# Low parts of six weight units: a negation on ScalarE and an adding transfer in the place of a subtraction on VectorE

## The chip, the cores and the metric

The kernel runs on one core of a Trainium2 chip. The core has five engines that run side by side and wait for one another by semaphores: TensorE (PE) multiplies matrices, VectorE (DVE) and ScalarE (ACT) work elementwise, GpSimd (POOL) does small elementwise work and issues transfers, and SyncE (SP) issues transfers. Sixteen DMA engines carry the transfers of all queues. The metric is the device time of one execution in microseconds, as the median of several runs.

## The reference, cut to what matters

Two decoder layers over 512 tokens of width 1024, all in float32. Each layer is an attention part and a gated feed-forward part with a causal convolution of width 3:

```python
def conv_ffn(h, w_up, conv_w, conv_b, w_down):
    u = causal_dwconv(h @ w_up, conv_w, conv_b)
    gate, up = jnp.split(u, 2, axis=-1)
    return (jax.nn.silu(gate) * up) @ w_down

for i in range(DEPTH):                       # DEPTH = 2
    ...                                      # attention part, x = x + rms_norm(h, post_g)
    h = conv_ffn(rms_norm(x, ffn_pre_g[i]), ffn_w_up[i], ffn_conv_w[i], ffn_conv_b[i], ffn_w_down[i])
    x = x + rms_norm(h, ffn_post_g[i])
```

The up projection `h @ w_up` has 1024 x 5632 weights: 22 blocks of 128 gate channels and 22 of 128 up channels. The down projection has 2816 x 1024.

## The kernel before

**Split numbers.** A float32 product is made of three matmuls. Every operand is held as a high part, which is the value rounded to the float32r type, and a low part, which is the value less its high part. `mm3` (L380 to L386) issues high by high (L384), low by high (L385 here, by operand order) and high by low (L386). So each weight needs two tiles, `wh` and `wl`, of 128 x 1024.

**Weight units.** The class `Weights` takes the weights in a fixed list of units. A unit is first loaded by SP into a raw tile `wraw` (`load`, L56), then split. ScalarE writes the high part with a copy that rounds, VectorE writes the low part with one subtraction. Where a unit is made in one go (`_emit` and `split`, L88 and L89) both stand together; in the feed-forward part the two steps are called apart, as `cast` (L100) and `low` (L111), at places written into the block's code, so that they fall between other work. `wh` and `wl` have five buffers each, `wraw` three (while some other tiles are free, five). A raw tile comes free when the subtraction has read it, and that lets SP issue the next load; SP issues its loads strictly in the order of the program.

**The up projection.** Of the 22 pairs of blocks in a layer, positions 4 to 19 are made by a scheme of seven products from sums of blocks (`seven`), whose weight sums POOL makes beforehand in HBM by adding transfers. Positions 0 to 3 and 20, 21 are plain: one unit for the gate block, one for the up block, 24 matmuls of 512 columns each (`plain`). Each pair is then convolved by `evict`: ScalarE scales (L506), VectorE adds the other two taps from PSUM (L510), ScalarE takes the silu (L515), VectorE multiplies (L519, L530). Sums and differences of the results (L537 to L544) and their high and low parts (`gh`, L548, and `gl`, L552) feed the down projection.

**The down projection** works on eleven pairs of weight blocks. For each pair SP loads a whole block `a` and one half of a second block `b` (L411). VectorE makes three differences of them (L404, L404, L407), and both are then split (L88, L89). The first difference reads both loads:

```python
sub(b[:, hi], b[:, lo], a[:, hi])     # L404, needs both loads
sub(a[:, hi], a[:, hi], a[:, lo])
add(b[:, lo], b[:, hi], a[:, lo])     # L407
```

**Order.** Outside of a few hand-written stretches a scheduler sets the order in which each engine gets its instructions when the program is built. Each engine then runs its list strictly in order. Tile names with numbers (`wl_5121`) are single buffers of one unit; a number names the same thing on all engines of one program.

**The stretch of this case** is the end of the up projection in each layer: at about 380 to 440 us in layer 0 and 890 to 950 us in layer 1. There the last block of seven products, the four plain units of positions 20 and 21, and the first units of the down projection follow each other. In layer 0 of the kernel before, the four plain units are `wh_5086`, `wh_5120`, `wh_5190` and `wh_5196` with their low parts.

Of the kernel before, what the change touches and what calls it, by code (L numbers as in the profile page):

```python
# [9 lines left out]
F32 = mybir.dt.float32  # L10
F32R = mybir.dt.float32r
BF16 = mybir.dt.bfloat16
AF = mybir.ActivationFunctionType
ALU = mybir.AluOpType
# [24 lines left out]
SEVEN = range(4, 20), range(4, 20)  # L39
# [6 lines left out]
class Weights:  # L46
# [7 lines left out]
        self.extra = []  # L54

    def load(self, raw=None):  # L56
        src, w = self.units[len(self.raws)]
        if raw is None and len(self.raws) % 5 < len(self.extra):
            raw = self.extra[len(self.raws) % 5]
        if raw is None:  # L60
            raw = self.raw_pool.tile([P, 1024], F32, tag="wraw", name="wraw", bufs=3)
        if isinstance(src, tuple):
            for n, part in enumerate(src):
                self.nc.sync.dma_start(raw[:, n * S:(n + 1) * S], part())
        else:
            self.nc.sync.dma_start(raw[:, :w], src)
        self.raws.append(raw)

    def _emit(self):
        n = len(self.made)  # L70
        if callable(self.units[n]):
            self.raws.append(None)
            self.made.append(self.units[n]())
            return
        if len(self.raws) == n:
            self.load()
        w = self.units[n][1]
        raw, self.raws[n] = self.raws[n], None
        h, l = self.pair()
        self.split(h, l, raw, w)  # L80
        self.made.append((h, l))

    def pair(self):
# [3 lines left out]
    def split(self, h, l, raw, w):  # L87
        self.nc.scalar.copy(h[:, :w], raw[:, :w])  # L88
        self.nc.vector.tensor_tensor(l[:, :w], raw[:, :w], h[:, :w].bitcast(F32), ALU.subtract)  # L89

    def cast(self):
        n = len(self.made) + len(self.open)
        if callable(self.units[n]):
            self.open.append(None)
            return
        if len(self.raws) == n:
            self.load()
        h, l = self.pair()
        w = self.units[n][1]
        self.nc.scalar.copy(h[:, :w], self.raws[n][:, :w])  # L100
        self.open.append((h, l, w))

    def low(self):
        unit = self.open.pop(0)
        if unit is None:
            self._emit()
            return
        h, l, w = unit
        n = len(self.made)
        raw, self.raws[n] = self.raws[n], None  # L110
        self.nc.vector.tensor_tensor(l[:, :w], raw[:, :w], h[:, :w].bitcast(F32), ALU.subtract)  # L111
        self.made.append((h, l))

    def ahead(self, n):
# [11 lines left out]
def trunk(tc, A, out):  # L126
# [3 lines left out]
    with ExitStack() as top:  # L130
# [79 lines left out]
        def up_blocks(layer):  # L210

            def block(i, j):
                if j < 4:
                    return A[f"ffn_up_q{layer}"][j, i * P:(i + 1) * P]
                c, i = PLACE[layer][i]
                return sums_of[layer][j - 4][c][i * P:(i + 1) * P]

            parts = [lambda i=i, j=j: block(i, j)
                     for i, j in ([(0, 0)] + [(i + (j == 0), j) for i in range(PAIRS[layer])
                                              for j in (4, 1, 5, 0, 6, 7, 3)]) if i < PAIRS[layer]]  # L220
            return [(tuple(parts[n:n + 2]), S * len(parts[n:n + 2])) for n in range(0, len(parts), 2)]

        def ffn_units(layer):
            up = []
            for f in range(NF):
                if f == SEVEN[layer][0]:
                    up += up_blocks(layer)
                elif f not in SEVEN[layer]:
                    up += [(A["ffn_w_up"][layer, f, z], 1024) for z in range(2)]
            return (up + [lambda n=n: down[layer](n) for n in range(4 * HF)])  # L230

        down, later_sums = {}, []
# [5 lines left out]
        for h in range(1, 4):  # L238
            units += [(A["ev_w_dqk"][h, z], 1024) for z in range(2)]
        units += [(A["ev_w_out"][k], 1024) for k in range(3, KD)]  # L240
        units += ffn_units(0)
        units += [(A["od_w_v"][u], 1024) for u in range(4)]
        units += [(A["od_w_sqk"][u], 1024) for u in range(4)]
        units += [(A["od_w_dqk"][u], 1024) for u in range(4, 12)]
        units += [(A["od_w_dqk"][u], 1024) for u in range(4)]
        units += [(A["od_w_v12"][u], 1024) for u in range(4)]
        units += [(A["od_w_out"][k], 1024) for k in range(2, 4)]
        units += ffn_units(1)
        W = Weights(nc, wpool, units, 5)

# [204 lines left out]
        def ffn(layer, xnT, pending, written, final):  # L455
            with ExitStack() as es:
# [126 lines left out]
                def seven(n, last):  # L583
# [15 lines left out]
                    if heavy:  # L599
                        cast()  # L600
                        tap(1, 1)
                        tap(0, 2)
                        ACT.copy(p5, p)
                        low()
                        silu()
                        cast()
                        tap(1, 2)
                    else:
                        ACT.copy(p5, p)
                        low()  # L610
                        cast()
                        tap(0, 2)
                        silu()
                        tap(1, 1)
# [3 lines left out]
                    if heavy:  # L618
                        rest[0]()
                        cast()  # L620
                    else:
                        tap(1, 2)
                        cast()
                        low()
# [1778 lines left out]
```

## Time and profile before

| | |
|---|---|
| median of 3 runs | 1041.91 us (1041.2 to 1042.88) |
| profiled execution | 1040.69 us, of which the span of the profile is 1038.9 us |
| PE busy | 1029.5 us, 99% |
| DVE busy | 900.9 us, 87% |
| ACT busy | 655.0 us, 63% |
| POOL busy | 124.4 us, 12% |
| granted TensorE clock | 0.999 |
| transfers | 217.26 MB, mean 209 GB/s |
| low parts by VectorE | x112 at 1218 ns (L89, two shapes) and x132 at 1219 ns (L111) |

Matmuls are pipelined: a 512-column matmul is shown with about 380 ns, but the next one starts about 216 ns after it, so a lost time of PE shows in the distance between two starts, and less than the full loss is shown as idle. An elementwise instruction that follows another without a wait starts some 90 ns before the former's shown end. "Idle before" names the event that ended the wait last. Transfers are shown at their issue, with the time from issue to landing.

### The profile page before, as it was taken

How to read it: one execution, taken by the hardware profiler on the slowest of the kernel's cores; microseconds unless marked ns; L12 is line 12 of the kernel's file. 1: busy time of each engine (PE TensorE's matmuls, PEld its weight loads, DVE VectorE, ACT ScalarE, POOL GpSimd, SP SyncE). 2: the span in 40 equal slices, each digit the busy share in tenths (PEclk: the TensorE clock that was granted, in tenths of full speed). 3: DMA queues.
4: the chain of work that ended last, by engine and by line, in shares of the span. 5: the costliest groups of instructions: out<-in, count | busy, mean ns of one | idle time of the engine just before them, and what ended most of it. 6: DMA issues, size and time to landing. Idle time of an engine off the chain costs nothing.

```text
span 1038.9 us, 18116 instructions
## 1 busy us (share of the span) xinstructions
PE 1029.5 (99%) x6736; PEld 934.9 (90%) x6736; DVE 900.9 (87%) x1542; ACT 655.0 (63%) x1129; POOL 124.4 (12%) x245
## 2 busy tenths in 40 slices
PE   9999999999999999999999999999999999999997
PEld 9878888899999999888888888899999999988886
DVE  7998786599999999999984775659999999999897
ACT  7676676466777766647654654656667776656562
POOL 3211144221000000000032111014100000000002
PEclk9999999999999999999999999999999999999999
DMA  7897999468665564455528999678986646545452
GB/s 281 268 246 217 263 303 277 131 222 229 202 195 164 191 182 154 154 168 180 211 79 296 281 292 290 209 221 269 270 235 211 187 161 204 163 134 180 151 214 82
DMA packets 72746, 217.26 MB, mean 209 GB/s; under 512 B 10065, under 2 KB 11217, under 8 KB 64465
## 3 DMA queue, kind: packets, MB, share of 16 engines
q1 hardware_dynamic: 61728, 147.55, 41.9%
q0 software_dynamic: 9920, 67.12, 25.0%
q10 hardware_dynamic: 1008, 1.43, 0.5%
q8 instruction: 53, 0.87, 0.3%
q14 instruction: 37, 0.30, 0.1%
HBM read 208.69 MB, written 73.43 MB: 272 GB/s over the span
## 4 chain that ended last, share of the span: by engine, by line
PE 88%; DVE 8%; issue 2%; ACT 1%; POOL 0%; DMA 0%; POOLq 0%; DVEq 0%; ACTq 0%
PE u L385 11%; PE u L384 11%; PE u L386 10%; PE acc L385 5%; PE acc L386 5%; PE acc L384 5%; PE apt L384 3%; PE apt L385 3%; PE apt L386 3%; DVE wl L89 2%; PE ao L384 2%; PE ao L386 2%; PE ao L385 2%; DVE y L510 2%; PE aqk L384 1%
## 5 line engine op out<-in xcount | busy, mean ns | idle before, releaser
L384 PE MATMUL u<-xh,wh 128*128 128x256 f32 (+1 forms) x640 | 189.8, 297 | 0.3 <-ACT wh L100 0.3
L385 PE MATMUL u<-xl,wh 128*128 128x256 f32 (+1 forms) x640 | 189.6, 296 | 0.0
L386 PE MATMUL u<-xh,wl 128*128 128x256 f32 (+1 forms) x640 | 189.3, 296 | 0.0
L89 DVE TENSOR_TENSOR wl<-wraw,wh 128x1024 fp32r<-128x1024 f32 (+1 forms) x112 | 135.0, 1218 | 33.7 <-ACT wh L88 33.5
L111 DVE TENSOR_TENSOR wl<-wraw,wh 128x1024 fp32r<-128x1024 f32 x132 | 159.4, 1219 | 1.5 <-ACT wh L100 1.5
L88 ACT CAST wh<-wraw 128x1024 fp32r<-128x1024 f32 (+1 forms) x112 | 115.0, 1044 | 58.6 <-PE apt L385 11.8
L100 ACT CAST wh<-wraw 128x1024 fp32r<-128x1024 f32 x132 | 136.9, 1044 | 22.6 <-PE u L385 6.9
L510 DVE SCALAR_TENSOR_TENSOR y<-u,cw,y 128x511 f32<-128x511 f32 (+1 forms) x176 | 126.1, 744 | 1.7 <-ACT y L506 0.7
L384 PEld LDWEIGHTS u<-xh,wh 128*128 128x128 f32 x640 | 122.5, 191 | 4.2 <-ACT wh L100 0.9
L385 PEld LDWEIGHTS u<-xl,wh 128*128 128x128 f32 x640 | 122.5, 191 | 3.9 <-DVE xl L316 0.4
L386 PEld LDWEIGHTS u<-xh,wl 128*128 128x128 f32 x640 | 122.5, 191 | 3.4
L384 PE MATMUL u<-gh,wh 128*128 128x256 f32 x384 | 105.7, 275 | 0.0
L385 PE MATMUL u<-gl,wh 128*128 128x256 f32 x384 | 105.6, 275 | 0.0
L386 PE MATMUL u<-gh,wl 128*128 128x256 f32 x384 | 105.6, 275 | 0.0
L385 PE MATMUL acc<-wl,gh 128*128 128x512 f32 (+1 forms) x234 | 88.6, 379 | 0.1
L384 PE MATMUL acc<-wh,gh 128*128 128x512 f32 (+1 forms) x234 | 88.4, 378 | 0.1
L386 PE MATMUL acc<-wh,gl 128*128 128x512 f32 (+1 forms) x234 | 88.3, 377 | 0.0
L506 ACT ACTIVATE y<-u,cw 128x512 f32<-128x512 f32 x88 | 66.6, 776 | 31.1 <-PE u L386 29.4
L265 POOL TENSOR_TENSOR rv<-ms,epst 128x1 f32<-128x1 f32 x31 | 8.6, 276 | 566.4 <-ACT junk L333 269.6
L384 PEld LDWEIGHTS u<-gh,wh 128*128 128x128 f32 x384 | 73.7, 192 | 0.2 <-DVE u L617 0.2
L385 PEld LDWEIGHTS u<-gl,wh 128*128 128x128 f32 x384 | 73.7, 192 | 0.0
L386 PEld LDWEIGHTS u<-gh,wl 128*128 128x128 f32 x384 | 73.7, 192 | 0.0
(418 smaller groups left out, 2532.7 us busy)
## 6 DMA issues: line engine op xcount, KB each, us to landing
ws<-in_ffn_up_q POOLq DMA_DIRECT2D x48, 768.0 KB, 13.0
wraw<-ws SPq DMA_DIRECT2D x128, 256.0 KB, 3.0
wraw<-in_ffn_up_q SPq DMA_DIRECT2D x96, 256.0 KB, 3.0
wraw<-in_ffn_w_down SPq DMA_DIRECT2D x44, 512.0 KB, 3.5
ws<-ws POOLq DMA_DIRECT2D x16, 768.0 KB, 13.0
ws<-in_ffn_up_q POOLq DMA_DIRECT2D x24, 512.0 KB, 6.9
wraw<-in_ffn_w_up SPq DMA_DIRECT2D x24, 512.0 KB, 4.8
wraw<-in_od_w_dqk SPq DMA_DIRECT2D x12, 512.0 KB, 9.5
```

Source lines behind the costliest of these rows:

```text
L88: self.nc.scalar.copy(h[:, :w], raw[:, :w])
L89: self.nc.vector.tensor_tensor(l[:, :w], raw[:, :w], h[:, :w].bitcast(F32), ALU.subtract)
L100: self.nc.scalar.copy(h[:, :w], self.raws[n][:, :w])
L111: self.nc.vector.tensor_tensor(l[:, :w], raw[:, :w], h[:, :w].bitcast(F32), ALU.subtract)
L265: POOL.tensor_tensor(v[:, :n], ms, eps[:, :n], ALU.add)
L384: PE.matmul(o, lh, rh, start=first, stop=False, skip_group_check=more)
L385: PE.matmul(o, lh, rl, start=False, stop=False, skip_group_check=more)
L386: PE.matmul(o, ll, rh, start=False, stop=last, skip_group_check=more)
L506: ACT.activation(y[:, z], u[z], AF.Identity, bias=c[:, 3:4], scale=c[:, 2:3])
L510: DVE.scalar_tensor_tensor(y[:, z, d:], u[z][:, :S - d], c[:, 2 - d:3 - d], y[:, z, d:], ALU.mult, ALU.add)
```

## The change

For units 41, 42 and 43 of each layer's up projection (the up block of position 20 and both blocks of position 21) the low part is no longer made by VectorE. ScalarE makes the high part as before. Then it writes the negated high part into the low tile, and POOL issues a transfer that reads the same weights from HBM a second time and adds them into the low tile. The values are the same: the low part is the weight less its high part. Unit 40, the gate block of position 20, is left as it was.

```diff
@@ class Weights
     def _emit(self):
...
         h, l = self.pair()
-        self.split(h, l, raw, w)
+        if len(self.units[n]) > 2:
+            self.send(n, h, l, raw)
+        else:
+            self.split(h, l, raw, w)
...
+    def send(self, n, h, l, raw):
+        src, w = self.units[n][:2]
+        self.nc.scalar.copy(h[:, :w], raw[:, :w])
+        self.nc.scalar.activation(l[:, :w], h[:, :w].bitcast(F32), AF.Identity, scale=-1.0)
+        self.nc.gpsimd.dma_start(l[:, :w], src, accum_op=ALU.add)
     def cast(self):
...
-        self.nc.scalar.copy(h[:, :w], self.raws[n][:, :w])
+        if len(self.units[n]) > 2:
+            self.send(n, h, l, self.raws[n])
+            w = 0
+        else:
+            self.nc.scalar.copy(h[:, :w], self.raws[n][:, :w])
         self.open.append((h, l, w))
     def low(self):
...
-        self.nc.vector.tensor_tensor(l[:, :w], raw[:, :w], h[:, :w].bitcast(F32), ALU.subtract)
+        if w:
+            self.nc.vector.tensor_tensor(l[:, :w], raw[:, :w], h[:, :w].bitcast(F32), ALU.subtract)
@@ def ffn_units(layer)
-                    up += [(A["ffn_w_up"][layer, f, z], 1024) for z in range(2)]
+                    sent = [("sent",) if n > 2 * SEVEN[layer][-1] + 2 else () for n in (2 * f, 2 * f + 1)]
+                    up += [(A["ffn_w_up"][layer, f, z], 1024, *sent[z]) for z in range(2)]
```

All lines below the class move down by up to 15 in the changed program, so L404 there is L419, L411 is L426, L510 is L525, L552 is L567.

The first place is ScalarE at the end of the up projection of layer 0, where the high parts of the last three units are made. Before:

```order
L100 CAST wh_5120<-wraw_5118 128x1024
L88 CAST wh_5190<-wraw_5188 128x1024
L506 ACTIVATE y_5066<-u_5001,cw_2662 128x512
L548 CAST gh_5164<-y_4684 128x1024
L506 ACTIVATE y_5066<-u_5002,cw_2662 128x512
L88 CAST wh_5196<-wraw_5194 128x1024
```

Of the change:

```order
L96 CAST wh_5120<-wraw_5118 128x1024
L97 ACTIVATE wl_5121<-wh_5120 128x1024
L96 CAST wh_5191<-wraw_5189 128x1024
L97 ACTIVATE wl_5192<-wh_5191 128x1024
L521 ACTIVATE y_5066<-u_5001,cw_2662 128x512
L563 CAST gh_5165<-y_4684 128x1024
L521 ACTIVATE y_5066<-u_5002,cw_2662 128x512
L96 CAST wh_5198<-wraw_5196 128x1024
L97 ACTIVATE wl_5199<-wh_5198 128x1024
```

Each of the three casts is followed by its negation; the rest keeps its order.

The second place is VectorE over the same time, from the low part of unit 40 (`wl_5087`) to the first difference of the down projection's weights (`wraw_5231` before, `wraw_5234` in the change). Before:

```order
L111 TENSOR_TENSOR wl_5087<-wraw_5084,wh_5086 128x1024
L519 TENSOR_TENSOR y_4935<-y_4935 128x512
L634 TENSOR_TENSOR u_5002<-u_5002,y_5066 128x256
L111 TENSOR_TENSOR wl_5121<-wraw_5118,wh_5120 128x1024
L89 TENSOR_TENSOR wl_5191<-wraw_5188,wh_5190 128x1024
L552 TENSOR_TENSOR gl_5165<-y_4684,gh_5164 128x1024
L510 SCALAR_TENSOR_TENSOR y_5066<-u_5001,cw_2662,y_5066 128x511
L89 TENSOR_TENSOR wl_5197<-wraw_5194,wh_5196 128x1024
L510 SCALAR_TENSOR_TENSOR y_5066<-u_5001,cw_2662,y_5066 128x510
L510 SCALAR_TENSOR_TENSOR y_5066<-u_5002,cw_2662,y_5066 128x511
L404 TENSOR_TENSOR wraw_5231<-wraw_5231,wraw_5229 128x512
```

Of the change:

```order
L125 TENSOR_TENSOR wl_5087<-wraw_5084,wh_5086 128x1024
L534 TENSOR_TENSOR y_4935<-y_4935 128x512
L649 TENSOR_TENSOR u_5002<-u_5002,y_5066 128x256
L567 TENSOR_TENSOR gl_5166<-y_4684,gh_5165 128x1024
L525 SCALAR_TENSOR_TENSOR y_5066<-u_5001,cw_2662,y_5066 128x511
L419 TENSOR_TENSOR wraw_5234<-wraw_5234,wraw_5232 128x512
L525 SCALAR_TENSOR_TENSOR y_5066<-u_5001,cw_2662,y_5066 128x510
L525 SCALAR_TENSOR_TENSOR y_5066<-u_5002,cw_2662,y_5066 128x511
```

The three subtractions are gone, and the first difference of the down projection now stands two taps earlier.

The third place is SP's list of loads: the four last loads of the up projection and the first of the down projection, with what each waits for (a raw tile that comes free). Before:

```order
L66 DMA wraw_5188<-in_ffn_w_up 128x1024 [waits DMAHW0_49,DMAHW7_49,DVE_49,Activation_49]
L66 DMA wraw_5194<-in_ffn_w_up 128x1024 [waits DMAHW1_49,DVE_49]
L411 DMA wraw_5229<-in_ffn_w_down 128x1024 [waits DMAHW2_49,DVE_49]
L411 DMA wraw_5231<-in_ffn_w_down 128x512 [waits DMAHW3_49,DVE_49]
L411 DMA wraw_5305<-in_ffn_w_down 128x1024 [waits DMAHW4_49,DVE_49]
```

Of the change:

```order
L66 DMA wraw_5189<-in_ffn_w_up 128x1024 [waits DMAHW0_49,DMAHW7_49,DVE_49,Activation_49]
L66 DMA wraw_5196<-in_ffn_w_up 128x1024 [waits DMAHW2_49,Activation_49]
L426 DMA wraw_5232<-in_ffn_w_down 128x1024 [waits DMAHW1_49,DVE_49]
L426 DMA wraw_5234<-in_ffn_w_down 128x512 [waits DMAHW3_49,Activation_49]
L426 DMA wraw_5308<-in_ffn_w_down 128x1024 [waits DMAHW4_49,Activation_49]
```

The order is the same, but the load of the last up unit waits for the cast of `wh_5120`, that of `wraw_5232` for the subtraction of `wl_5087`, and the next two for the casts of `wh_5191` and `wh_5198`.

More of the change, by code (lines that the diff above doesn't have):

```diff
@@ L56, in load @@
     def load(self, raw=None):
-        src, w = self.units[len(self.raws)]
+        src, w = self.units[len(self.raws)][:2]
         if raw is None and len(self.raws) % 5 < len(self.extra):
```

## The prediction

> **What bounds the kernel now.** The chain of waits comes first, and behind it the busy shares:
>
> ```profile
> PE 1029.5 (99%) x6736; PEld 934.9 (90%) x6736; DVE 900.9 (87%) x1542; ACT 655.0 (63%) x1129; POOL 124.4 (12%) x245
> PE 88%; DVE 8%; issue 2%; ACT 1%; POOL 0%; DMA 0%; POOLq 0%; DVEq 0%; ACTq 0%
> ```
>
> PE ends nearly every wait. To gain time, the change has to remove idle time of PE; to lose time it has only to make some. So I read the stretch of the change by engine (length, PE, PEld, DVE, ACT, POOL with counts, then granted clock, DMA share, GB/s), two windows in each layer:
>
> ```profile
> 398.00:424.00 26.00, 25.70 (x141) 22.78 (x140) 24.92 (x35) 14.58 (x20) 0.00 (x0) 1.00 0.37 129
> 424.00:450.00 26.00, 25.95 (x120) 22.12 (x119) 25.86 (x36) 15.34 (x19) 0.00 (x0) 1.00 0.54 178
> 905.00:931.00 26.00, 26.00 (x142) 23.13 (x142) 24.99 (x37) 14.76 (x20) 0.00 (x0) 1.00 0.39 130
> 931.00:957.00 26.00, 25.89 (x119) 22.06 (x119) 25.86 (x36) 15.26 (x19) 0.00 (x0) 1.00 0.52 179
> ```
>
> DVE is as full as PE, with 0.14 us free in 26 from 424 on. ACT has 11 us free, POOL all, the clock is full, and the DMA engines are busy for half of the time or less. The next question is how much PE loses behind the change. In its timeline (start, length) I looked for starts further apart than 0.216 us:
>
> ```profile
> 428.29 0.38 PE L386 MATMUL acc<-wh,gl 128*128 128x512 f32 x1
> 428.65 0.45 PE L384 MATMUL acc<-wh,gh 128*128 128x512 f32 x1
> 428.94 0.38 PE L385 MATMUL acc<-wl,gh 128*128 128x512 f32 x1
> 439.74 0.38 PE L384 MATMUL acc<-wh,gh 128*128 128x512 f32 x1
> 440.17 0.48 PE L385 MATMUL acc<-wl,gh 128*128 128x512 f32 x1
> 440.49 0.38 PE L386 MATMUL acc<-wh,gl 128*128 128x512 f32 x1
> ```
>
> From 428.29 to 428.94 two starts take 0.65 instead of 0.43: 0.22 lost. From 439.74 to 440.49 they take 0.75: 0.32 lost. That is 0.53 us in layer 0, and the same two places of layer 1 (935.6 and 947.1) lose 0.61 by the same sum. Both end on DVE, the first on a tap and the second on a low part:
>
> ```profile
> 427.76 0.74 DVE L510 SCALAR_TENSOR_TENSOR y<-u,cw,y 128x510 f32<-128x510 f32 x1
> 438.89 1.22 DVE L89 TENSOR_TENSOR wl<-wraw,wh 128x1024 fp32r<-128x1024 f32 x1
> ```
>
> So **all that an earlier DVE can give here is 1.1 us**, a tenth of a per cent. In the other direction there is no such bound: its 1.1 us of idle time in the first window (26.00 less 24.92) all lie ahead of 404.5, so each microsecond by which DVE is late behind that point comes out at PE near 428 (935 in layer 1).
>
> **What goes away.** Three subtractions per layer, here with what stands between them (VectorE, layer 0):
>
> ```profile
> 402.00 1.22 DVE L111 TENSOR_TENSOR wl<-wraw,wh 128x1024 fp32r<-128x1024 f32 x1
> 403.13 1.22 DVE L89 TENSOR_TENSOR wl<-wraw,wh 128x1024 fp32r<-128x1024 f32 x1
> 404.50 1.23 DVE L552 TENSOR_TENSOR gl<-y,gh 128x1024 fp32r<-128x1024 f32 x1
> 405.64 0.74 DVE L510 SCALAR_TENSOR_TENSOR y<-u,cw,y 128x511 f32<-128x511 f32 x1
> 406.30 1.22 DVE L89 TENSOR_TENSOR wl<-wraw,wh 128x1024 fp32r<-128x1024 f32 x1
> 407.44 1.40 DVE L510 SCALAR_TENSOR_TENSOR y<-u,cw,y 128x510 f32<-128x510 f32 x2
> 408.75 0.68 DVE L404 TENSOR_TENSOR wraw<-wraw 128x512 f32<-128x512 f32 x1
> ```
>
> Three times 1.14 us (403.13 to the next start it allows, 406.30 to 407.44) would be 3.4 us. Two of the three stand ahead of `gl`, and `gl` needs `gh` of ACT:
>
> ```profile
> 401.30 1.05 ACT L88 CAST wh<-wraw 128x1024 fp32r<-128x1024 f32 x1 [1.80 <-PE u L385]
> 402.76 0.78 ACT L506 ACTIVATE y<-u,cw 128x512 f32<-128x512 f32 x1 [0.41 <-PE u L386]
> 403.44 1.03 ACT L548 CAST gh<-y 128x1024 fp32r<-128x1024 f32 x1
> ```
>
> The cast at 401.30 is let go by PE, which the change doesn't move. A negation now follows it. It is not in the trace; the nearest row is the cast of the same shape, 1.04 us. So: cast to 402.35, negation to 403.4, scaling 0.68, `gh` from some 404.0 to 405.05, `gl` at 405.07, which is 0.57 later than before. Then the tap (1.14 later) and 0.66 later, at **406.87**, the first difference of the down weights, L419. Before, two taps of 1.31 us together stood ahead of it, so 408.75 less 1.31 = **407.44** is the start at which all behind runs as before. The lead is 0.57 us. In layer 1 the same sum goes from these rows (ACT, then DVE):
>
> ```profile
> 908.12 1.05 ACT L88 CAST wh<-wraw 128x1024 fp32r<-128x1024 f32 x1 [1.93 <-PE u L385]
> 911.44 1.22 DVE L552 TENSOR_TENSOR gl<-y,gh 128x1024 fp32r<-128x1024 f32 x1
> 915.68 0.68 DVE L404 TENSOR_TENSOR wraw<-wraw 128x512 f32<-128x512 f32 x1
> ```
>
> `gl` comes at about 911.9, L419 at 913.7, and even is 914.37: a lead of 0.7. Both leads are larger than what PE loses in their layer, so with the loads in time the gain would be those 0.53 + 0.61 = 1.1 us.
>
> **The loads of L419.** It reads two loads of SP: 512 KB, then 256 KB. Before, they took (issue, us to landing):
>
> ```profile
> wraw<-in_ffn_w_down SPq DMA_DIRECT2D x1, 512.0 KB, 4.2
> ```
> ```profile
> wraw<-in_ffn_w_down SPq DMA_DIRECT2D x1, 256.0 KB, 3.7
> ```
>
> They were issued at 403.24 and 404.38, and the second landed at 408.1, 0.6 us ahead of L404. Now the first waits for the subtraction of `wl_5087` (it ends at 401.15), the second for the cast that ends at 402.35 (909.17 in layer 1). At 3.7 us the second would be there at 406.1, in time.
>
> But just then POOL's three new transfers of 512 KB are under way: they are issued behind the negations, the first at some 400.9, the second at 403.7. What an adding transfer does to a load beside it is shown earlier in the program, where POOL makes weight sums. First such a transfer alone, then a load alone, then two fences with both beside each other, and a window that counts the packets of the two queues (packets, MB, share of the time):
>
> ```profile
> ws<-in_ffn_up_q POOLq DMA_DIRECT2D x1, 512.0 KB, 5.3
> ```
> ```profile
> wraw<-ws SPq DMA_DIRECT2D x1, 256.0 KB, 2.7
> ```
> ```profile
> ws<-in_ffn_up_q POOLq DMA_DIRECT2D x1, 512.0 KB, 6.7
> wraw<-ws SPq DMA_DIRECT2D x1, 256.0 KB, 6.6
> ```
> ```profile
> ws<-in_ffn_up_q POOLq DMA_DIRECT2D x1, 512.0 KB, 8.0
> wraw<-ws SPq DMA_DIRECT2D x1, 256.0 KB, 4.8
> wraw<-in_ffn_up_q SPq DMA_DIRECT2D x1, 256.0 KB, 7.2
> ```
> ```profile
> q0 software_dynamic: 49, 0.39, 79.0%
> q1 hardware_dynamic: 43, 0.08, 9.5%
> ```
>
> A load of 256 KB alone takes 2.7 (at 300 us); beside adding transfers 6.6 (at 230.5), 4.8 and 7.2 (at 744). In the window, 2.75 us at 766, the two queues get about as many packets, 49 and 43, but POOL's hold the engines for 79% of the time and SP's for 9.5%. A load gets one small packet for each long one. I take 6.6 to 7.2 us for the second load, by the two rows nearest in kind (256 KB, beside adding transfers that follow one another): from the end of the cast at 402.4 it lands at 402.4 + 6.6 to 7.2 = 409.0 to 409.6, **1.6 to 2.2 us late**; in layer 1 at 915.8 to 916.4, 1.4 to 2.0 late. The bounds are 3.7 (in time) and 8.0 (3.0 and 2.8 late).
>
> This is the place for a rule. The Trainium skill, *DMA: Bandwidth & Descriptors*, section *Queues, rings and completion order*, has each engine take turns between the queues that have work, packet by packet; 49 against 43 agrees. It speaks against the change. By that rule, with new packets of half the length of those at 766 (an estimate), the second load would land near 410.3, and the sum would be about 5.5 in place of 3.6.
>
> What DVE then loses: it waits at L419, and the two taps behind it, which gave PE no trouble, and all that follows come as late as L419 does, 1.9 and 1.7 us in the middle. No idle time of DVE is left until 450 to take it back, so PE stops near 428 and near 935 for that much more.
>
> **The adding transfers themselves.** An addition into on-chip memory isn't in the trace. The bounds are the plain load, 4.2, and the 8.0 above. PE uses the first such low part here, in its first L386:
>
> ```profile
> 408.64 0.38 PE L385 MATMUL u<-xl,wh 128*128 128x512 f32 x1
> 408.86 0.38 PE L386 MATMUL u<-xh,wl 128*128 128x512 f32 x1
> ```
>
> From 400.9 that allows 8.0 us: enough by all rows, barely by the longest. The second is due at about 414.0, the third at 419.2, with 10 us or more each. I take nothing for it.
>
> **At nothing.** The negations (3 of 1.04 per layer) lie in ACT's free time but for the 0.57 counted above; without that cover they would cost 3.1 per layer. POOL's issues, 0.8 each in such rows, have an idle POOL under them; a busy one would push each transfer by its issue. SP's load of the last up unit goes 1.6 us earlier, and nobody waits for it. PE's order is the same.
>
> **The sum.** 1040.69 of the profiled execution + 1.9 + 1.7 = 1044.3; the median of the runs is 1.22 above that execution, so 1045.5. This case's own range is 1043.5 (0.8 late in each layer, a load of 5.8 us) to 1048 (a load of 8.0 in both layers: 1040.69 + 3.0 + 2.8 + 1.22 = 1047.7).
>
> **Rivals.**
> *A gain.* The loads aren't held back: both land in the time before 407.44 and 914.37, that is within 5.0 us. For it speaks the row of 4.8, one of three loads beside adding transfers, and that the first load leaves 2 us earlier. Against it speak 6.6 and 7.2. PE's 1.1 us at the four places go: 1040.8.
> *No change.* The loads are late by 0 to 1 us: the lead is gone and little more. This needs 5.0 to 6.0 us, between the rows. 1041.9 to 1043.9, in the middle 1042.5.
> *The adding transfer is the stall.* If an addition into on-chip memory lasts 12 us under three of its kind and the loads, PE waits at 408.86 for 4 us in each layer (the point from which it decides is 8 us); DVE's lateness hides under that. 1041.9 + 8 = 1050. For it speaks the 8.0; against it, that in the rows the longest also had company.
> The first of these is the one on the other side: one mechanism, decided at L419, with its point at 5.0 us.
>
> **How the numbers follow.** Loads held back 0.50; gain 0.14; no change 0.24; adding transfer late 0.12. A measurement of this kernel tells some 0.2%, 2.1 us, from no change. The gain of 0.1% would read as no change, so faster gets only 0.05. The rest of the gain (0.09), the no-change case (0.24) and 0.04 from the lower end of the first case make 0.37 for the same. The rest of the first case (0.46) and the last rival (0.12) make 0.58 for slower. The range from 1040.7 to 1048.6 holds the gain's value, no change, and the first case with its upper bound; it leaves out most of the last rival above and some of the gain below, together no more than 0.2.
>
> **What would show it.** In the groups: L125 with 130 instructions in place of 132, L92 with 108 in place of 112. In the table of transfers a row of six from the up weights into `wl` on POOL's queue, with 6 to 8 us; at 12 the last rival is right. DVE idle for about 3 us ahead of `gl`, put down to ACT; then L419 idle for about 2 us twice, put down to the load of the down weights. If L419 starts at 406.9 without a wait, the gain is right and PE's stalls near 428.6 and 440.2 are gone; if PE waits at 408.9 for a transfer of POOL's, the last rival. PE otherwise loses some 2 us near 430 and near 937. Wrong altogether would be a total above 1050 or a stall ahead of 400.

## The result, and the profile after

The change makes the kernel slower: **1054.6 us** median of 5 runs (1052.33 to 1056.93) against 1041.91 us (1041.18 to 1043.19), a ratio of 1.0122 (95% interval 1.0107 to 1.0138), or 12.7 us. The forecast was 1045.5, with a range up to 1048.6: the side was right, the size was not.

The profiled execution took 1056.51 us, with a span of 1054.7. Its busy shares, then the transfers that the change adds, from the table of DMA issues (count, KB each, median us from issue to landing):

```profile
PE 1034.0 (98%) x6736; PEld 938.3 (89%) x6736; DVE 895.8 (85%) x1536; ACT 661.0 (63%) x1135; POOL 129.3 (12%) x251
```
```profile
wl<-in_ffn_w_up POOLq DMA_DIRECT2D x6, 512.0 KB, 9.3
```

Six instructions less on DVE, six more on ACT and on POOL, as written. The transfers take 9.3 us in the middle, above the 8.0 that the prediction had as their upper bound. The groups show the subtractions of the weights down to 130 and 108:

```profile
L125 DVE TENSOR_TENSOR wl<-wraw,wh 128x1024 fp32r<-128x1024 f32 x130 | 156.9, 1219 | 1.8 <-ACT wh L113 1.7
L92 DVE TENSOR_TENSOR wl<-wraw,wh 128x1024 fp32r<-128x1024 f32 (+1 forms) x108 | 130.0, 1216 | 32.9 <-ACT wh L91 32.5
```

VectorE's timeline in layer 0, around the first difference of the down weights, and then the same instruction in layer 1:

```profile
401.85 0.43 DVE L649 TENSOR_TENSOR u<-u,y 128x256 f32<-128x256 f32 x1
405.19 1.23 DVE L567 TENSOR_TENSOR gl<-y,gh 128x1024 fp32r<-128x1024 f32 x1 [2.91 <-ACT gh L563]
406.34 0.74 DVE L525 SCALAR_TENSOR_TENSOR y<-u,cw,y 128x511 f32<-128x511 f32 x1
413.08 0.69 DVE L419 TENSOR_TENSOR wraw<-wraw 128x512 f32<-128x512 f32 x1 [6.00 <-DMA wraw<-in_ffn_w_down]
```
```profile
928.32 0.69 DVE L419 TENSOR_TENSOR wraw<-wraw 128x512 f32<-128x512 f32 x1 [7.03 <-DMA wraw<-in_ffn_w_down]
```

The 2.9 us of idleness ahead of `gl` and the wait for the load of the down weights are where the prediction put them; the wait is 6.0 and 7.0 us long and not 2. TensorE's timeline shows what becomes of it:

```profile
409.79 0.48 PE L401 MATMUL u<-xh,wl 128*128 128x512 f32 x1 [0.64 <-DMA wl<-in_ffn_w_up]
...
428.79 0.46 PE L399 MATMUL acc<-wh,gh 128*128 128x512 f32 x1 [1.69 <-DVE y L525]
...
434.44 0.45 PE L399 MATMUL acc<-wh,gh 128*128 128x512 f32 x1 [2.82 <-DVE y L525]
```

First a short wait for the first transferred low part, then two waits for taps that VectorE does late. And behind the second one the granted clock falls to half, which no rival had (windows; columns as in the prediction):

```profile
434.00:436.00 2.00, 1.56 (x6) 1.40 (x7) 1.90 (x5) 0.00 (x0) 0.00 (x0) 0.88 0.69 258
436.00:438.00 2.00, 2.00 (x6) 1.55 (x6) 1.97 (x4) 1.70 (x2) 0.00 (x0) 0.50 0.38 131
438.00:440.00 2.00, 2.00 (x9) 1.69 (x8) 2.00 (x2) 2.00 (x4) 0.00 (x0) 0.77 0.44 135
```

TensorE runs the same 6736 matmuls in the same order in all kernels here, so the start of the n-th matmul in one profile less that of the n-th before gives the shift at every place. The steps of that shift, in us:

| step, at its time in the kernel before | layer 0 | layer 1 |
|---|---|---|
| wait for the first transferred low part (409; 916) | 0.91 | 1.66 |
| the two waits for late taps (429; 936) | 5.04 | 5.23 |
| half clock behind them | 1.40 | 1.37 |
| stall of the kernel before that is gone (440; 947) | -0.32 | -0.32 |

That is 15.0 of the 15.8 us by which the two profiles differ. (The profiled execution of the change was 1.9 us above its median, that of the kernel before 1.2 below.) A second profile of the change (e11_change_again, below) has the two waits for late taps in both layers and the half clock in layer 1 only.

### The profile page after: what moved, and what is told of

Read it like the earlier page. It is cut to its first block, busy times and chain, and to the rows that moved or that the text cites. A ratio compares the mean times of both kernels' runs of the same rounds, so it can differ in the third digit from the quotient of the medians.

```text
span 1054.7 us, 18121 instructions
## 1 busy us (share of the span) xinstructions
PE 1034.0 (98%) x6736; PEld 938.3 (89%) x6736; DVE 895.8 (85%) x1536; ACT 661.0 (63%) x1135; POOL 129.3 (12%) x251
## 4 chain that ended last, share of the span: by engine, by line
PE 43%; DVE 3%; DMA 1%; issue 1%; ACT 1%; POOL 1%; POOLq 0%; DVEq 0%; ACTq 0%
PE u L399 5%; PE u L400 5%; PE u L401 5%; PE acc L399 3%; PE acc L400 3%; PE acc L401 3%; PE apt L399 3%; PE apt L400 3%; PE apt L401 3%; PE apv L399 1%; PE apv L401 1%; PE apv L400 1%; DMA wraw<-in_ffn_w_down 1%; DVE wl L92 1%; PE p L400 1%
## 5 line engine op out<-in xcount | busy, mean ns | idle before, releaser
L125 DVE TENSOR_TENSOR wl<-wraw,wh 128x1024 fp32r<-128x1024 f32 x130 | 156.9, 1219 | 1.8 <-ACT wh L113 1.7
L92 DVE TENSOR_TENSOR wl<-wraw,wh 128x1024 fp32r<-128x1024 f32 (+1 forms) x108 | 130.0, 1216 | 32.9 <-ACT wh L91 32.5
L91 ACT CAST wh<-wraw 128x1024 fp32r<-128x1024 f32 (+1 forms) x108 | 111.1, 1044 | 61.1 <-PE apt L400 11.7
L525 DVE SCALAR_TENSOR_TENSOR y<-u,cw,y 128x511 f32<-128x511 f32 (+1 forms) x176 | 126.0, 744 | 1.3 <-ACT y L521 0.4
L205 POOL DMA_DIRECT2D ws<-in_ffn_up_q x72 | 50.4, 722 | 166.0 <-DMA ws<-ws 61.4
## 6 DMA issues: line engine op xcount, KB each, us to landing
ws<-in_ffn_up_q POOLq DMA_DIRECT2D x48, 768.0 KB, 12.7
ws<-ws POOLq DMA_DIRECT2D x16, 768.0 KB, 12.4
```

Source lines behind the costliest of these rows:

```text
L205: nc.gpsimd.dma_start(tiles[j][c][:].rearrange(wide, q=4), src.rearrange(wide, q=4), accum_op=op, max_dma_last_dim=8192)
L525: DVE.scalar_tensor_tensor(y[:, z, d:], u[z][:, :S - d], c[:, 2 - d:3 - d], y[:, z, d:], ALU.mult, ALU.add)
```

## The experiments

Two theories stood against each other in the first runs: **A**, the transfers fill the DMA engines and the down loads come late; **B**, the negations ahead of `gh` and the moved VectorE list cost the time. **C** says that it is the addition, not the bytes, that makes a transfer so costly. The kernel before was run beside each set (1042.18, 1042.38, 1042.09 and 1041.73 us).

| run | median, us | ratio to before (95% interval) |
|---|---|---|
| e1_no_transfer | 1044.18 | 1.0022 (1.0012 to 1.0031) |
| e2_plain_copy | 1046.52 | 1.0040 (1.0026 to 1.0055) |
| e3_transfer_only | 1056.95 | 1.0138 (1.0123 to 1.0153) |
| e4_half_bytes | 1047.59 | 1.0060 (1.0039 to 1.0080) |
| e5_transfer_only | 1050.14 | 1.0075 (1.0061 to 1.0089) |
| e6_nothing_instead | 1043.07 | 1.0007 (0.9998 to 1.0017) |
| e7_last_unit_only | 1044.45 | 1.0020 (1.0011 to 1.0029) |
| e8_pool_subtracts | 1051.93 | 1.0095 (1.0079 to 1.0112) |
| e9_adds_behind_loads | 1050.19 | 1.0078 (1.0058 to 1.0097) |
| e10_first_unit_only | 1046.83 | 1.0036 (1.0021 to 1.0050) |
| e11_change_again | 1055.61 | one run |
| e12_behind_loads_again | 1049.03 | one run |

**e1_no_transfer.** The transfers are left out.

```diff
@@ send
-        self.nc.gpsimd.dma_start(l[:, :w], src, accum_op=ALU.add)
```

> The change without its six transfers: the three negations per layer stay, VectorE's three subtractions stay out, and the low part of the three units is left as the negated high part, so part of the computation is left out. Theory A (the transfers fill the DMA engines from 403 to 416 us, and the down loads behind or beside them come 6 us late): the first difference L419 starts at some 406.9 without a wait, PE's stalls at 428 and 434 go, and the time is 1040.8 (1040 to 1042). Rival B (the negation ahead of gh and the moved VectorE list are the cost, the transfers only look guilty): most of the loss stays, 1048 or more. Rival C (the addition, not the bytes, is the cost): as A.

Measured: 1044.18. With the transfers about 10 of the 12.7 us go, so B is not the larger part. In layer 0 the loads take 3.4 and 3.2 us (rows of DMA issues), and L419, here L418, starts behind its tap without a wait (in layer 1 after one of 0.48 us):

```profile
wraw<-in_ffn_w_down SPq DMA_DIRECT2D x1, 512.0 KB, 3.4
wraw<-in_ffn_w_down SPq DMA_DIRECT2D x1, 256.0 KB, 3.2
```
```profile
405.69 0.74 DVE L524 SCALAR_TENSOR_TENSOR y<-u,cw,y 128x511 f32<-128x511 f32 x1
406.36 0.68 DVE L418 TENSOR_TENSOR wraw<-wraw 128x512 f32<-128x512 f32 x1
```

But A had 1040.8 here, and the run is 2 us slower than before. The gain didn't come; e6 takes that up.

**e2_plain_copy.** The same transfers without the addition.

```diff
@@ send
-        self.nc.gpsimd.dma_start(l[:, :w], src, accum_op=ALU.add)
+        self.nc.gpsimd.dma_start(l[:, :w], src)
```

> The change with the six transfers as plain copies, without the addition: same bytes from HBM, same place, same issue; the low part of these units is the whole weight, so the values are others. Theory A (bytes): the second down load again lands some 10 us after its issue, L419 waits for 5 to 6 us, and the time is 1051 to 1056. Rival B: the same. Rival C (the read and write back of an addition makes a packet long, 350 ns for 4 KB): packets fall to half, L419 waits 1 to 2 us, 1043 to 1046.

Measured: 1046.52. A in its plain form (bytes) is wrong; C is right, though the time is half a microsecond above its range. The same stretch of 15 us in the three kernels, as a window (its last columns are the DMA share and GB/s) with the two queues (packets, MB, share). Before:

```profile
401.00:416.00 15.00, 15.00 (x85) 13.50 (x84) 14.85 (x23) 9.44 (x12) 0.00 (x0) 1.00 0.37 123
```
```profile
q1 hardware_dynamic: 576, 1.84, 37.1%
```

The change:

```profile
401.00:416.00 15.00, 14.36 (x81) 12.65 (x80) 6.08 (x10) 7.91 (x10) 2.61 (x3) 1.00 0.95 225
```
```profile
q0 software_dynamic: 423, 1.56, 54.9%
q1 hardware_dynamic: 560, 1.79, 39.2%
```

And with plain copies:

```profile
401.00:416.00 15.00, 15.00 (x87) 13.58 (x87) 11.43 (x18) 11.14 (x15) 1.68 (x3) 1.00 0.73 229
```
```profile
q1 hardware_dynamic: 576, 1.84, 40.3%
q0 software_dynamic: 432, 1.57, 32.0%
```

POOL's queue (q0) moves the same bytes in both but for a last few packets, 1.57 and 1.56 MB. As copies a packet takes 32.0% of 16 x 15 us over 432, 0.18 us; as additions 54.9% over 423, 0.31 us. (Both counts hold some 45 packets of a few bytes; those of 4 KB alone take 0.20 and 0.34 us in the mean.) The additions bring the engines from 0.37 to 0.95 of their time, the copies to 0.73. The second down load takes 5.1 us with copies where it takes 10.5 with additions, and L419 waits 0.62 and 1.83 us in the two layers.

**e3_transfer_only.** The kernel before, with three adding transfers per layer into unused memory.

```diff
@@ class Weights, called behind the cast of units 41 to 43
+    def extra_add(self, n, h):
+        ...
+            self.nc.gpsimd.tensor_copy(self.tiny[:, :1], h[:, :1].bitcast(F32))
+            self.nc.gpsimd.dma_start(s[:, :1024], self.units[n][0], accum_op=ALU.add)
```

> The kernel before, whole, plus the same reads of 512 KB, three per layer, as adding transfers of POOL into unused HBM memory, each let go by the cast of its unit through a one-column copy on POOL. VectorE's and ScalarE's lists are those of before. Theory A: the two first down loads, 4.2 and 3.7 us before, take 8 to 11 us, L404 waits some 5 us in each layer, and the time is 1049 to 1055. Rival B: 1042. Rival C: as A.

Measured: 1056.95, and it tells nothing of the stretch: nothing tied the transfers to the copies ahead of them, and four of the six were put at the start of the program, where TensorE lost 9.8 us waiting for its inputs. (A wait of 5.1 us there also went with a half clock, from 12.4 to 19.2 us.) e5 repeats it.

**e4_half_bytes.** Each adding transfer over half of the columns.

```diff
@@ send
-        self.nc.gpsimd.dma_start(l[:, :w], src, accum_op=ALU.add)
+        self.nc.gpsimd.dma_start(l[:, :w // 2], src[:, :w // 2], accum_op=ALU.add)
```

> The change with each of the six transfers over the left half of its columns only (256 KB); the right half of the low parts is left as the negated high part. Theory A: 0.75 MB less per layer in the same stretch, at about 0.2 MB per us some 3.7 us less queueing: L419 waits for 1.5 to 3 us in the place of 6, no wait of PE for the first low part, no second long stall and so no low clock; 1043.5 to 1047. Rival B: 1052 to 1055, as the whole. Rival C: as A.

Measured: 1047.59, 0.6 above A's range. The queue's row, in the same window:

```profile
q0 software_dynamic: 432, 0.79, 31.9%
```

Half the bytes as additions hold the engines for as long as all the bytes as copies (31.9% and 32.0%), and the two kernels cost much the same: 1.0060 and 1.0040, with intervals that overlap. So the cost fits the engines' time better than the bytes, and an addition takes 1.7 (4 KB packets) to 2 times (2 KB packets) as much of that time per byte as a copy.

**e5_transfer_only.** As e3, with the transfers of units 42 and 43 tied behind their copies; that of unit 41 stayed behind its copy in both. All add into HBM memory, not into the low tiles.

```diff
@@ extra_add
-            self.nc.gpsimd.dma_start(s[:, :1024], self.units[n][0], accum_op=ALU.add)
+            with (self.tc.issue_after(c.ins) if ordered else ExitStack()):  # c: the copy; ordered: units 42, 43
+                self.nc.gpsimd.dma_start(s[:, :1024], self.units[n][0], accum_op=ALU.add)
```

> The kernel before, whole, plus three adding transfers of 512 KB per layer from the same weights into unused HBM memory, each behind a one-column copy on POOL that waits for the cast of its unit. This time each transfer is tied behind its copy (in e3_transfer_only four of the six ran at the start of the program). Theory A (the adding transfers fill the DMA engines: a 4 KB packet takes 330 ns where a plain one takes 160 to 175): the first down loads take 8 to 10 us in place of 4.2 and 3.7, L404 waits for 4 to 5 us in each layer, 1050 to 1056. Rival B (negations and the moved VectorE list are the larger part): 1042 to 1044.

Measured: 1050.14, with VectorE's whole old list and no negation. So the transfers alone make the kernel 8 us slower. In the profiled execution 1.7 us of it is a half clock in layer 1, from 942.4 to 945.9, behind a stall of 3.4 us. The way is not quite the one that A gave. L404, here L416, waits only 1.07 us, and a late up load, by way of ScalarE's cast, had made VectorE wait 1.38 just ahead of it (1.36 and 1.75 in layer 1):

```profile
408.26 1.23 DVE L90 TENSOR_TENSOR wl<-wraw,wh 128x1024 fp32r<-128x1024 f32 x1 [1.38 <-ACT wh L89]
...
411.87 0.69 DVE L416 TENSOR_TENSOR wraw<-wraw 128x512 f32<-128x512 f32 x1 [1.07 <-DMA wraw<-in_ffn_w_down]
```

The first down load took 4.7 us and the second 6.7, where A had 8 to 10; 6.7 is inside the 6.6 to 7.2 that the prediction took for it. Here the first load is issued 3.6 us behind the first transfer (403.89 against 400.30), in the change 0.3 (401.37 against 401.11). The rest of the change's loss, 4 to 5 us, goes with what e5 hasn't: the change's own order of loads and VectorE work and its negations, which cost 2.0 us without any transfer (e1), and the waits for low parts that come by transfer. No run here separates these further.

**e6_nothing_instead.** The high part stands in for the low part; no negation, no transfer.

```diff
@@ send
-        self.nc.scalar.activation(l[:, :w], h[:, :w].bitcast(F32), AF.Identity, scale=-1.0)
-        self.nc.gpsimd.dma_start(l[:, :w], src, accum_op=ALU.add)
@@ cast (and _emit)
             self.send(n, h, l, self.raws[n])
-            w = 0
+            l, w = h, 0
```

> The change without negations and without transfers: the high part stands in for the low part of the three units, so part of the computation is left out; VectorE has three subtractions less per layer and ScalarE nothing more. If the later gh is what kept e1_no_transfer at 1044.2: 1040.8, the gain of 1.1. If the new order of VectorE's list behind it (a difference more ahead of the low part that PE waits for at 440 us) and the loop of loads from 446 us on take the lead back: 1042 to 1044.5, as e1_no_transfer.

Measured: 1043.07, a ratio of 1.0007 (0.9998 to 1.0017). So even with the three subtractions removed and nothing in their place there is no gain. By the shift of the matmuls TensorE does gain 0.49 us at the two stalls of layer 0 (428 and 440) and 0.29 at the first of layer 1; by 520 us 0.77 has been given back in layer 0, and 0.6 in layer 1. The first place is a wait for a later down load, on VectorE, then TensorE's for the low part made of it:

```profile
463.59 0.69 DVE L418 TENSOR_TENSOR wraw<-wraw 128x512 f32<-128x512 f32 x1 [1.83 <-DMA wraw<-in_ffn_w_down]
```
```profile
466.61 0.48 PE L399 MATMUL acc<-wl,gh 128*128 128x512 f32 x1 [0.29 <-DVE wl L93]
```

In the kernel before the same difference waits 1.48 us and TensorE doesn't. From 446 us on loads, differences and low parts run in a loop through a few raw tiles. That a list arranged anew for the earlier part meets this loop in another way is the likely cause; no run tests it. The negations may add some more: e1 less e6 is 1.1 us, but their intervals overlap.

**e7_last_unit_only** and **e10_first_unit_only.** The change for one unit of the three.

```diff
-                    sent = [("sent",) if n > 2 * SEVEN[layer][-1] + 2 else () for n in (2 * f, 2 * f + 1)]
+                    ... n > 2 * SEVEN[layer][-1] + 4 ...      # e7: unit 43
+                    ... n == 2 * SEVEN[layer][-1] + 3 ...     # e10: unit 41
```

> The change for unit 43 alone: one negation, one adding transfer, one subtraction less per layer. The transfer is issued at some 407, when the first two down loads have nearly landed. Theory A: those two take 4 to 5 us as before, only the third load is beside the transfer and is due 10 us later; no long stall, no low clock: 1041 to 1044. If any adding transfer in this stretch holds back a load that matters: 1046 or more. For a version that beats the kernel before it would have to come out below 1041.

> The change for unit 41 alone: one negation, one adding transfer, one subtraction less per layer. One addition beside the loads. Theory A: it lands 6 to 7 us after its issue, PE waits 0 to 0.5 us for the first low part where the whole change makes it wait 0.9 and 1.6; the first difference isn't late by more than 1.5 us; 1042 to 1046. If the first transfer alone brings the stalls: above 1049.

Measured: 1044.45 and 1046.83, each a little above the upper end that theory A gave it (by 0.45 and 0.83). Neither beats the kernel before. With the last unit alone the loads are in time but for 0.25 us (0.72 in layer 1), TensorE loses nothing at 428, and the loss stands behind 440 us as in e6. With the first unit alone the two loads take 7.4 and 5.5 us and L419 waits 0.36 and 1.32 us:

```profile
410.58 0.69 DVE L419 TENSOR_TENSOR wraw<-wraw 128x512 f32<-128x512 f32 x1 [0.36 <-DMA wraw<-in_ffn_w_down]
```

**e8_pool_subtracts.** POOL makes the low part from the raw tile and the high part.

```diff
@@ send
-        self.nc.scalar.activation(l[:, :w], h[:, :w].bitcast(F32), AF.Identity, scale=-1.0)
-        self.nc.gpsimd.dma_start(l[:, :w], src, accum_op=ALU.add)
+        self.nc.gpsimd.tensor_tensor(l[:, :w], raw[:, :w], h[:, :w].bitcast(F32), ALU.subtract)
```

> The change with a subtraction by POOL in the place of each negation and transfer: VectorE has three subtractions less per layer, no bytes are added, ScalarE has nothing more, and the low parts are whole. POOL's subtraction isn't in the trace; for 1024 columns I allow 1.5 to 3 us. Theory A: no load is late, 1041 to 1044.5 like e6_nothing_instead. If POOL's subtraction and VectorE's work disturb each other, or the raw tile is held so long that the loads come late: 1046 or more.

Measured: 1051.93, the second outcome, at a place of its own: TensorE waits 3.5 us up to 406.9 and 3.3 up to 919.7 for VectorE, and behind both waits the clock is at half for 3.4 us (from 407.3 and from 919.3). The two timelines, POOL and then VectorE:

```profile
400.28 2.37 POOL L97 TENSOR_TENSOR wl<-wraw,wh 128x1024 fp32r<-128x1024 f32 x1 [147.82 <-ACT wh L96]
403.12 2.81 POOL L97 TENSOR_TENSOR wl<-wraw,wh 128x1024 fp32r<-128x1024 f32 x1 [0.47 <-ACT wh L96]
```
```profile
400.46 3.27 DVE L124 TENSOR_TENSOR wl<-wraw,wh 128x1024 fp32r<-128x1024 f32 x1
403.65 2.83 DVE L533 TENSOR_TENSOR y<-y 128x512 f32<-128x512 f32 x1
```

A subtraction of 1.22 us on VectorE is shown with 3.27, a product of 0.69 with 2.83: they end 1.08 and 0.55 us behind POOL's beside them, which is nearly the time that each takes alone. The Trainium skill, *SBUF — State Buffer*, section *Who interferes with whom*, has it that a VectorE instruction with two inputs in SBUF and a GpSimd one that reads SBUF exclude each other. These rows agree.

**e9_adds_behind_loads** and **e12_behind_loads_again.** The second and third transfer of each layer wait until the second down load has landed.

```diff
@@ send
-        self.nc.gpsimd.dma_start(l[:, :w], src, accum_op=ALU.add)
+        if n % 2 == 0 or self.late:
+            self.late.append((l[:, :w], src))
+        else:
+            self.nc.gpsimd.dma_start(l[:, :w], src, accum_op=ALU.add)
+    def flush(self, b):                # b: the tile of the second down load
+        c = self.nc.gpsimd.tensor_copy(self.tiny[:, :1], b[:, :1])
+        with self.tc.issue_after(c.ins):
+            for l, src in self.late:
+                self.nc.gpsimd.dma_start(l, src, accum_op=ALU.add)
```

> The whole change, with the second and third adding transfer of each layer held until the second down load has landed (POOL copies one column of it first). Same bytes, same additions, same lists of VectorE and ScalarE; only the first addition is beside the loads. If the meeting of the down loads with two or three additions is what makes L419 5.7 us late: the second load takes 5 to 7 us in place of 10.5, L419 waits for 0 to 1.5 us, PE instead waits a little for the second low part (due at some 414, landing at 414 to 416); 1044 to 1049. If the loads are late for another reason, or the additions cost the same wherever they are: 1052 to 1056 again.

> e9_adds_behind_loads profiled a second time. There one addition beside the loads made the second load take 9.1 us, where e10_first_unit_only with one addition had 5.5. If that is the rule for loads issued beside the addition: 8 to 10 us again; if it was an odd execution: 5 to 7 us, and a wait of L419 below 2 us.

Measured: 1050.19 and, in the second profile, 1049.03; at and a little above the upper end of what the first theory expected, and 4 to 6 us below the change. In layer 0 the second load took 9.1 us and then 6.8, and L419, here L431, waited 4.66 and 2.35 (in layer 1 2.99 and 3.72):

```profile
411.83 0.69 DVE L431 TENSOR_TENSOR wraw<-wraw 128x512 f32<-128x512 f32 x1 [4.66 <-DMA wraw<-in_ffn_w_down]
```
```profile
409.25 0.69 DVE L431 TENSOR_TENSOR wraw<-wraw 128x512 f32<-128x512 f32 x1 [2.35 <-DMA wraw<-in_ffn_w_down]
```

So one addition beside the two loads is enough for waits of 2 to 5 us here, and of 0.36 and 1.32 in e10, and two executions of one program differ in layer 0 by 2.3 us, more than the forecast's whole term of 1.9. Neither expectation for the second profile holds as it stands: its load is as short as an odd first profile would have it, and its wait is above 2 us. Holding back the others helps, and moves the wait: TensorE now waits about 2 us in each layer for the held transfers, and in layer 0 of the first profile 1.9 us for the one that wasn't held, which took 10.0 us.

**e11_change_again.** No edit.

> The change as it is, profiled a second time, to see how far one profile speaks for the others. If the late loads are the rule: the second down load again takes 8 to 11 us, L419 waits for 4 to 6 us in layer 0, and the time is 1052 to 1057. If the first profile was an odd one: 6.6 to 7.2 us, a wait of about 2 us, and a time below 1050.

Measured: 1055.61. The second down load takes 9.3 us, and L419 waits 4.86 and 5.93 us:

```profile
412.42 0.69 DVE L419 TENSOR_TENSOR wraw<-wraw 128x512 f32<-128x512 f32 x1 [4.86 <-DMA wraw<-in_ffn_w_down]
...
927.95 0.69 DVE L419 TENSOR_TENSOR wraw<-wraw 128x512 f32<-128x512 f32 x1 [5.93 <-DMA wraw<-in_ffn_w_down]
```

The late loads are in both profiles. The half clock comes and goes: in layer 0 a stall of 2.98 us, up to 433.8, is followed by full clock, and in layer 1 one of 2.09, up to 943.7, by half a clock from 944.6 to 948.0. The first transferred low part landed in 7.4 us in layer 0, and TensorE didn't wait for it there. And this execution lost 3.1 us in small pieces between 440 us and the same stretch of layer 1, where e1 lost 1.5, e6 1.1 and the first profile of the change nothing.

## Why the prediction was right in its mechanism and wrong in its size

**The bound and the way of the loss: right.** Loads of the down weights held back by POOL's additions, VectorE late at L419, TensorE stopping near 428 and 935: the trace has each of them, e1 shows that they go with the transfers, and e5 that transfers alone, without any other part of the change, cost 8 us. The lateness goes on to TensorE nearly one to one, as forecast: L419 starts at 413.08 where 407.44 plus TensorE's own shift of 0.12 was even, 5.52 late; TensorE lost 5.95 up to 430 (0.91 and 5.04). In layer 1 it is 6.44 late (928.32 against 914.37 + 7.51) and 6.89 lost.

**The step that failed: the second load's 6.6 to 7.2 us.** It took 10.5 in the first profile and 9.3 in the second, so the terms of 1.9 and 1.7 us measured 5.5 and 6.4. The rows were for loads of 256 KB, and the sum took the load by itself. Here it stands behind the end of the last up load and the first down load of 512 KB, and beside additions all the while. From its issue to its landing the engines have no time left (the two queues, 402.5 to 413.0 us):

```profile
q0 software_dynamic: 312, 1.15, 58.4%
q1 hardware_dynamic: 403, 1.21, 41.8%
```

Together that is all of the 10.5 us: 6.1 for additions and 4.4 for SP's 1.21 MB, of which the two down loads are 0.79. The windows that the prediction read, a share of 0.37 and 0.54, were averages of 26 us in which it all seemed to fit; what counts is the 6 us from the first load's issue, at 401.4, until L419's data are due, at 407.4. The prediction's upper bound, 8.0 us, was the row of a transfer of POOL's, and no bound. By the rule of turns between queues, which the prediction took from the Trainium skill, *DMA: Bandwidth & Descriptors*, section *Queues, rings and completion order*, its estimate was 410.3 for the landing; that is nearer to the measured 413.0 than its sum, and still short of it. Why one addition costs L419 2.35 us in one execution and 4.66 in another stays open.

**A term taken at nothing: the first low part.** Its bound of 8.0 us was passed: the transfer took 8.6 us, and 9.5 in layer 1, and TensorE waited 0.9 and 1.7 us. The rival of the late transfer was thus partly true. It seems to cost little of its own: a wait of TensorE at 409 leaves less of VectorE's lateness to wait for at 428, and the two steps of layer 0 together, 5.95, are little more than the 5.52 by which L419 was late.

**A term that was missing: the clock.** In the first profile TensorE ran at 0.50 for 3.4 us in each layer, which cost 2.8 us in all. Of the five executions of the change the two with a mean clock of 0.994 took 1056.5 and 1056.9 us, the three with 0.997 or 0.998 took 1052.3 to 1054.6. The length of the stall ahead doesn't decide it: stalls of 2.98 us in the first profile and one of 2.09 in the second were followed by half a clock, and one of 2.98 in the second, one of 2.8 in e5 and one of 2.08 in the first were not.

The Trainium skill, *TensorE: Matmul & The Clock Gate*, section *Part 1: The HAM clock gate*, has a free-running window of about 3.4 us whose idleness halves the clock. The traces agree with the window: the two half clocks of the first profile begin at 435.51 and 950.92 us, 151 times 3.413 apart, and each lasts 3.41. They don't agree with a window that has to be wholly idle. Here are the window ahead and the one at half clock, in layer 0 of the first profile and in layer 1 of the second (behind the length of 3.41 stands PE's busy time):

```profile
432.10:435.51 3.41, 1.07 (x5) 1.00 (x6) 3.27 (x6) 0.60 (x1) 0.00 (x0) 1.00 0.52 197
435.51:438.92 3.41, 3.41 (x10) 2.69 (x9) 3.38 (x6) 2.62 (x3) 0.00 (x0) 0.50 0.29 100
```
```profile
941.20:944.61 3.41, 1.49 (x8) 1.00 (x7) 3.41 (x6) 2.67 (x4) 0.00 (x0) 1.00 0.45 177
944.61:948.02 3.41, 3.41 (x9) 2.33 (x7) 3.38 (x6) 1.25 (x2) 0.00 (x0) 0.50 0.47 154
```

Away from the two ends of the program, every such window of a profile here that ran at full clock with PE busy for 1.49 us or less was followed by half a clock, and none with 1.50 or more. A stall across the border of two windows leaves work in both: in layer 0 of the second profile the two that hold the stall of 2.98 us have 1.76 and 2.24 us of it. So a stall of 2.1 us or more may bring 1.4 to 1.7 us with it, by where it falls. The stalls that the prediction forecast, 1.9 and 1.7, lie just below that.

**The gain that wasn't to be had.** The gain rival's 1.1 us (1040.8 with the loads in time) is wrong in itself. e6 takes the three subtractions out for nothing and ends at 1.0007. Its stalls at 428 and 440 in layer 0 and the first of layer 1 do go, and the time comes back, in layer 0 behind 446 us. The prediction counted TensorE's stalls at four places as if the lists behind them stayed as they were. What the change had to win was nothing that can be measured, and so all that it added was loss.

## What to carry to other kernels

Before work is moved into transfers, add up the DMA engines' time between the moment the data are issued and the moment they are due, with an addition counted nearly twice, and put the loads that must land in that stretch into the same sum; an average share of a longer window says little. And before anything is paid to relieve an engine, try the kernel with that work simply left out: here it would have shown at once that the relief is worth nothing. A wait that is longest in one profile should be looked at in a second one before it is explained to the last microsecond.

## What the runs showed of the hardware

- A packet of POOL's transfers took 0.31 us on average as an addition (423 packets, 54.9% of 16 engines for 15 us) and 0.18 as a copy (432 packets, 32.0%) from the same place to the same tiles, or 0.34 and 0.20 for the packets of 4 KB alone; the additions of 2 KB took as long as copies of 4 KB (432 packets, 31.9%).
- A load of 256 KB that takes 3.2 us without the additions (e1) took 10.5 beside them, behind another load of 512 KB, and the engines had no time left while it was under way (58.4% and 41.8%).
- A stall of TensorE of 2.1 to 3 us can be followed by half a clock for 3.41 us (435.51 to 438.92 us: 0.50), and need not be. In these traces it was when PE was shown busy for 1.49 us or less in one of the windows of 3.41 us at whose borders the clock changes.
- A POOL subtraction of 128 x 1024 takes 2.4 to 2.8 us beside VectorE's work, and a subtraction and a product of VectorE beside it stretch from 1.22 to 3.27 and from 0.69 to 2.83 us.
